# Six raw weight places instead of five, paid for by sharing two small tiles

## The chip, the cores and the metric

One Trainium2 chip, one of its cores. The metric is the device time of one launch in microseconds (us), median of the runs shown. Five engines run side by side, each through its own list of instructions: TensorE (PE; its weight loads are listed apart as PEld), VectorE (DVE), ScalarE (ACT), GpSimd (POOL) and SyncE (SP). In this kernel SP issues nearly all large loads from HBM, and 16 DMA engines carry them out.

## The reference

Two transformer blocks on 256 tokens of width 1024, in float32. The change lies in the last part of the first block, a mixture of 32 experts of which every token takes two:

```python
def expert_block(args):
    tok, wt, e = args
    xb = h_pad[tok]
    y = (jax.nn.silu(xb @ w_gate[e]) * (xb @ w_up[e])) @ w_down[e]
    return y * wt[:, None]
```

`w_gate[e]` and `w_up[e]` are 1024 x 512, `w_down[e]` is 512 x 1024, so each expert brings 6 MB of weights. Before this part come the modulation, attention and Fourier mixing and the router. After it come four feed-forward layers, an attention with selected keys and a gated MLP, all with weights that are read once.

## The kernel before

**Stream and places.** All weights are one list, `self.stream`, cut into pieces of at most 1 MB. `load` (L57 to L70) issues a piece from SP into a tile `raw` of the pool `rawp`. That pool has `RAW` = 5 places of 8 KB in each partition. `run_loads` (L78 to L82) decides how far ahead loads go:

```python
while self.loaded < len(self.stream) and self.loaded < self.free + RAW:
    self.load()
```

`self.free` is the first piece that is not yet done with its place. Pieces become done through `finished`, and `free` moves only over a run of done pieces. A piece that is held long therefore also holds back the loads that lie `RAW` places behind it, even if pieces after it are done. Which place a new piece gets is chosen when the program is built: the one that comes free earliest. SP runs its list in order, so a load that waits for its place holds up all loads behind it.

**Two ways of using a piece.** Most pieces are cut in two numbers of lower precision: ACT copies `raw` into `wh` (`high`, L104), DVE subtracts to get `wl` (`low`, L113), and the piece is finished. PE then multiplies with `wh` and `wl`. There are four pairs of `wh`/`wl` and one more pair (`whx`/`wlx`) in this stage. One piece of every expert, the second half of `w_down` (`NATIVE`), is not cut. PE multiplies with `raw` itself, and the place comes free only when these matmuls are done (`raw_done`).

**The expert stage.** Six pieces belong to an expert, in the order in which they are loaded: two of `w_gate` of expert e, two of `w_down` of expert e-1 (the second is the uncut one), two of `w_up` of expert e. In `moe` the order on PE, ACT and DVE is written out by hand (`tc.manual_schedule`). One pass e of the loop has on PE: first half of gate (`rows(e, 0, 0)`), the transposes of the up product of expert e-1 (`turn(1)`), `place`, second half of gate, `scatter` of expert e-2, both halves of down of expert e-1, first half of up, two pieces of `gather` (for e below 28 only), the transposes of the gate product (`turn(0)`), second half of up. The product of 64 slots x 512 comes out of PSUM as a copy by ACT (`leave`, L1517) into a tile `gu0` for gate or `gu1` for up, one buffer each. `turn` reads that tile on PE, and `total` on DVE adds what it left in PSUM. The product of silu(gate) and up is cut into `act` (two buffers), which `down` reads.

**The branch ahead of it.** Between the router and the expert stage there is a branch for experts with more than 64 tokens (`overflow`). SP reads a number for it (`TENSOR_LOAD most`, L1383) and waits there until the router has it. Loads behind the branch in SP's list cannot be issued earlier. The branch is not taken with these inputs.

**Elsewhere** the order on the engines is set by a scheduler, and the same `load` and `run_loads` feed the weights.

Of the kernel before, what the change touches and what calls it, by code (L numbers as in the profile page):

```python
# [10 lines left out]
F32 = mybir.dt.float32  # L11
F32R = mybir.dt.float32r
# [6 lines left out]
P = 128  # L19
# [1 line left out]
D = 1024  # L21
EPS = 1e-6
PIECE = 2048
RAW = 5
SX = 1
NEG = -1e30
SEL = -3e38
# [2 lines left out]
class Net:  # L30
    def __init__(self, ctx, tc, I, out):
        self.ctx, self.tc, self.nc, self.I, self.out = ctx, tc, tc.nc, I, out
        self.cp = self.pool(ctx, "const", 1)
        self.rawp = self.pool(ctx, "raw", RAW)
        self.psp = ctx.enter_context(tc.tile_pool(name="psum", bufs=4, space=PSUM))
# [42 lines left out]
    def run_loads(self):  # L78
        while self.free in self.done:
            self.done.discard(self.free)  # L80
            self.free += 1
        while self.loaded < len(self.stream) and self.loaded < self.free + RAW:  # L82
            self.load()
# [771 lines left out]
    def first(self):  # L855
# [3 lines left out]
        with ExitStack() as ctx:  # L859
# [171 lines left out]

            A, rec = {}, {}

            def scores(hd, t):
# [15 lines left out]
                nc.vector.scalar_tensor_tensor(p[0], p[1], st[:, 3, 1:2], p[0], op0=OP.mult, op1=OP.add)  # L1050
                A[hd, t] = p[0]

            def a_tr(hd, t):
                ps = self.bank().rearrange("p (k n) -> p k n", k=4)
                for kt in range(4):
                    nc.tensor.transpose(ps[:, kt, :], A[hd, t][:, P * kt : P * kt + P], self.idf)
                aT = at.tile([P, 4, P], F32, name="aT", bufs=2)
                nc.scalar.copy(aT, ps)
                A[hd, t] = aT

            O = {}

            def av(hd, t):
                if hd == 0:
                    O[t] = self.bank("acc").rearrange("p (h n) -> p h n", h=4)
                aT = A.pop((hd, t))
                for kt in range(4):
# [386 lines left out]
    def moe(self):  # L1454
        nc, tc, I = self.nc, self.tc, self.I
        self.limit = self.moe_end
        with ExitStack() as ctx:
            mp = self.pool(ctx, "moe", 1)
            self.extend(self.pool(ctx, "splitx", SX))
            XG, G, GT, gt, gu, act, ys, acc = {}, {}, {}, {}, {}, {}, {}, {}  # L1460

            def hot(g):
                G[g] = mp.tile([P, T, 4, P], F32R, name="G", bufs=2)
                for t in range(T):
                    nc.vector.tensor_tensor(G[g][:, t], self.slots[:, None, :].to_broadcast([P, 4, P]),
                                            self.posm[:, t, 4 * g : 4 * g + 4, None].to_broadcast([P, 4, P]),
                                            op=OP.is_equal)
# [16 lines left out]
            def place(e):  # L1484
                ps = gt[e] = self.bank().bitcast(F32R)
                for t in range(T):
                    nc.tensor.transpose(ps[:, P * t : P * t + P],
                                        G[e // 4][:, t, e % 4, :], self.idr)

            def grown(e):  # L1490
                ps = gt.pop(e)
                GT[e] = mp.tile([P, 256], F32R, name="GT", bufs=2)
                nc.scalar.copy(GT[e], ps[:, :256])
# [15 lines left out]
            def rows(e, which, q):  # L1509
                if q == 0:  # L1510
                    pr[which] = self.bank()
                product(pr[which], XG[e // 4][:, e % 4], None, piece(e, 2 * which + q), 4, 4 * q, 7)

            def leave(e, which):

                sb = mp.tile([P, 512], F32, name=f"gu{which}", bufs=1)
                nc.scalar.copy(sb.rearrange("s (a p) -> s a p", a=4), pr[which].rearrange("s (p a) -> s a p", a=4))  # L1517
                gu[which] = sb

            def turn(which):  # L1520
                tu[which] = self.bank()
                for a in range(4):
                    o = slice(P * a, P * a + P)
                    nc.tensor.transpose(tu[which][:, o], gu[which][:, o], self.idf)  # L1524

            def total(which):
                z[which] = mp.tile([P, 4, 64], F32, name=f"sum{which}", bufs=1)
                nc.vector.tensor_reduce(z[which], tu[which].rearrange("p (a i s) -> p a s i", a=4, i=2), axis=AX.X, op=OP.add)

            def down(e, q):  # L1530
                if q == 0:
                    pd[0], pd[1] = self.bank(), self.bank()
                w = piece(e, 4 + q)
                for half in range(2):
                    product(pd[half], act[e], None, w, 2, 2 * q, 3, slice(512 * half, 512 * half + 512))

            def yhigh(e, half):
                yh[half] = mp.tile([P, 512], F32R, name="yh", bufs=2)
                nc.scalar.activation(yh[half], pd[half], AF.Copy, scale=self.gslot[:, e : e + 1])

            def ylow(e, half):
                yl = mp.tile([P, 512], F32R, name="yl", bufs=2)
                nc.vector.scalar_tensor_tensor(yl, pd[half], self.gslot[:, e : e + 1], yh[half].bitcast(F32),  # L1543
                                               op0=OP.mult, op1=OP.subtract)
                ys.setdefault(e, []).append((yh[half], yl))

            def scatter(e):
                order = [(t, half) for half in range(2) for t in range(T)]
                for t, half in sorted(order) if e == 31 else order:
                    if e == 0:  # L1550
                        acc[t, half] = self.bank("acc")
                    for i in range(2):
                        self.mm(acc[t, half], GT[e][:, P * t : P * t + P], ys[e][half][i],
                                start=e == 0 and i == 0, stop=e == 31 and i == 1)
                del ys[e]
# [8 lines left out]
            def cut(which, e, n):  # L1564

                if (e, n) in names:
                    k = names.index((e, n)) + 1
                    while made[which] < k:
                        (self.low if which else self.high)()
                        made[which] += 1  # L1570
# [13 lines left out]
            with tc.manual_schedule(engines={mybir.EngineType.PE, mybir.EngineType.Activation, mybir.EngineType.DVE}):  # L1584
                for e in range(34):
                    new, old, last = e < 32, 0 < e < 33, e > 1
                    if new:
                        rows(e, 0, 0)
                    if old:
                        leave(e - 1, 1)  # L1590
                        nc.scalar.activation(z[0], z[0], AF.Silu)
                        cut(1, e - 1, 4)
                        turn(1)
                        place(e - 1)
                    cut(0, e, 2)
                    if old:
                        total(1)
                        nc.vector.tensor_mul(z[0], z[0], z[1])
                    if new:
                        rows(e, 0, 1)  # L1600
                    if old:
                        grown(e - 1)
                        A = act[e - 1] = mp.tile([P, 4, P], F32R, name="act", bufs=2)
                        self.split(A[:, :, :64], A[:, :, 64:], z[0])
                    if e % 4 == 0 and 0 < e < 28:
                        hot(e // 4 + 1)
                    cut(0, e, 3)
                    cut(1, e, 2)
                    if last:
                        scatter(e - 2)  # L1610
                    if new:
                        leave(e, 0)
                    if old:
                        down(e - 1, 0)
                    cut(0, e + 1, 0)
                    cut(1, e, 3)
                    if old:
                        down(e - 1, 1)
                    cut(0, e + 1, 1)
                    cut(1, e + 1, 0)  # L1620
                    if old:
                        self.raw_done()
                        for half in range(2):
                            yhigh(e - 1, half)
                            ylow(e - 1, half)
                    if new:
                        rows(e, 1, 0)
                    cut(0, e, 4)
                    cut(1, e + 1, 1)
                    if e < 28:  # L1630
                        for i in range(2):
                            gather(e // 4 + 1, 2 * (e % 4) + i)
                    if new:
                        turn(0)
                        total(0)
                        rows(e, 1, 1)
# [105 lines left out]
```

## Time and profile before

| | |
|---|---|
| Median of 3 runs | 1897.24 us (1896.63 to 1899.16) |
| Profiled execution, its own time | 1900.3 us |
| its span in the trace | 1898.6 us |
| PE busy | 1822.9 us, 96% |
| DVE busy | 1335.2 us, 70% |
| ACT busy | 1155.3 us, 61% |
| Expert stage, 237 to 760 us | 523 us: PE 505.27, DVE 448.07, ACT 409.60 us busy, DMA engines 0.95 of the time, 367 GB/s |
| A stretch of the second block, 900 to 1100 us | 200 us: PE 199.60, DVE 134.94, ACT 117.74 us busy, DMA engines 0.51, 170 GB/s |

The shares of busy time are averages over stages. The expert stage is one of heavy loads (367 GB/s), the second block is one of matmuls (PE busy all the time). The engine lists run in order, so an idle time in a list is ended by the thing that its next instruction waited for. The profile names this releaser.

### The profile page before, as it was taken

What the parts mean: (1) busy time and instruction counts of PE and PEld (TensorE: products, weight loads), DVE (VectorE), ACT (ScalarE), POOL (GpSimd) and SP (SyncE); (2) the same over time, 40 slices, a digit from 0 to 9 for tenths busy, and PEclk for the clock granted to TensorE, in tenths of its full rate; (3) what the DMA queues carried; (4) which work ended last, traced back from release to release, by engine and by line L of the source; (5) the groups of instructions that cost most, each with busy time, mean ns of one, the idle gap of its engine ahead of it and who ended that gap; (6) DMA issues with size and microseconds to landing.
All of it is one profiled execution on the core that took longest, in us unless ns stands there. A gap on an engine that the chain in (4) does not pass through costs nothing.

```text
span 1898.6 us, 23007 instructions
## 1 busy us (share of the span) xinstructions
PE 1822.9 (96%) x8305; PEld 1444.0 (76%) x8305; DVE 1335.2 (70%) x2114; ACT 1155.3 (61%) x1912; POOL 40.1 (2%) x73
## 2 busy tenths in 40 slices
PE   5999799999999999899999999999999999999998
PEld 2777577777777776688888888887888888887886
DVE  6887788888888888855577765556555776765554
ACT  6555588787777777744465664446444755465443
POOL 1000000000000000000000000000000010100000
PEclk8999799999999999999999999999999999999999
DMA  9774299999999999655564455555555555665551
GB/s 325 256 271 168 74 365 366 360 356 368 367 374 361 366 375 376 232 187 186 181 210 171 155 176 180 178 199 185 176 180 197 181 178 191 216 210 196 177 179 42
DMA packets 189268, 450.51 MB, mean 237 GB/s; under 512 B 9904, under 2 KB 118840, under 8 KB 164576
## 3 DMA queue, kind: packets, MB, share of 16 engines
q1 hardware_dynamic: 185056, 437.25, 64.3%
q0 software_dynamic: 3808, 11.25, 2.1%
q8 instruction: 66, 1.08, 0.2%
q10 hardware_dynamic: 288, 0.52, 0.1%
q14 instruction: 50, 0.41, 0.1%
HBM read 447.91 MB, written 1.07 MB: 236 GB/s over the span
## 4 chain that ended last, share of the span: by engine, by line
PE 72%; DMA 8%; ACT 5%; DVE 3%; issue 1%; SPq 0%; ACTq 0%; DVEq 0%
PE bank_w L161 51%; PE bank_acc L161 18%; DMA raw<-w_up 6%; ACT wh L104 2%; DMA raw<-w_down 2%; DVE wl L113 1%; PE bank_w L316 1%; PE bank_w L1524 1%; ACT wh L169 1%; PE bank_w L247 0%; ACT xh L250 0%; ACT XG L1482 0%; PE bank_w L719 0%; DVE yl L1543 0%; ACT L192 0%
## 5 line engine op out<-in xcount | busy, mean ns | idle before, releaser
L170 DVE TENSOR_TENSOR wl<-raw,wh 128x512 fp32r<-128x512 f32 (+3 forms) x814 | 522.9, 703 | 250.8 <-ACT wh L169 250.1
L169 ACT CAST wh<-raw 128x512 fp32r<-128x512 f32 (+3 forms) x814 | 461.1, 635 | 267.4 <-PE bank_w L161 204.0
L161 PE MATMUL bank_w<-wh,xh 128*128 128x512 f32 (+2 forms) x1056 | 407.0, 386 | 4.1 <-ACT xh L250 3.4
L161 PE MATMUL bank_w<-wh,xl 128*128 128x512 f32 (+2 forms) x1056 | 402.9, 382 | 0.9 <-DVE xl L251 0.9
L161 PE MATMUL bank_w<-wl,xh 128*128 128x512 f32 (+2 forms) x1056 | 402.5, 381 | 0.0
L104 ACT CAST wh<-raw 128x2048 fp32r<-128x2048 f32 x124 | 236.7, 1910 | 97.8 <-DMA raw<-w_up 47.5
L113 DVE TENSOR_TENSOR wl<-raw,wh 128x2048 fp32r<-128x2048 f32 x124 | 280.7, 2284 | 3.2 <-ACT wh L104 3.1
L161 PEld LDWEIGHTS bank_w<-wh,xh 128*128 128x128 f32 x1056 | 199.4, 189 | 42.7 <-ACT xh L250 6.3
L161 PEld LDWEIGHTS bank_w<-wh,xl 128*128 128x128 f32 x1056 | 199.1, 189 | 37.6 <-DVE xl L251 2.1
L161 PEld LDWEIGHTS bank_w<-wl,xh 128*128 128x128 f32 x1056 | 199.5, 189 | 35.1 <-issue 0.2
L161 PE MATMUL bank_w<-wh,XG 128*128 128x512 f32 x388 | 169.8, 438 | 0.0
L161 PE MATMUL bank_w<-wl,XG 128*128 128x512 f32 x388 | 152.3, 392 | 0.0
L161 PE MATMUL bank_acc<-wh,th 128*128 128x512 f32 x352 | 144.2, 410 | 0.0
L161 PE MATMUL bank_acc<-wh,tl 128*128 128x512 f32 x352 | 138.1, 392 | 0.0
L161 PE MATMUL bank_acc<-wl,th 128*128 128x512 f32 x352 | 137.9, 392 | 0.0
L309 ACT ACTIVATE silu<-bank_w,rs 128x256 f32<-128x256 f32 x88 | 41.7, 474 | 153.7 <-PE bank_w L161 153.5
L311 DVE SCALAR_TENSOR_TENSOR hid<-bank_w,rs,silu 128x256 f32<-128x256 f32 x88 | 42.6, 484 | 117.5 <-ACT silu L309 114.3
L161 PE MATMUL bank_w<-raw,act 128*128 128x512 f32 x256 | 115.0, 592 | 0.0
L161 PEld LDWEIGHTS bank_w<-wl,XG 128*128 128x128 f32 x388 | 73.1, 188 | 19.9 <-issue 7.2
L161 PEld LDWEIGHTS bank_w<-wh,XG 128*128 128x128 f32 x388 | 73.0, 188 | 19.9 <-issue 7.4
L161 PEld LDWEIGHTS bank_w<-raw,act 128*128 128x128 f32 x256 | 48.4, 189 | 48.5 <-issue 46.0
L161 PEld LDWEIGHTS bank_acc<-wh,tl 128*128 128x128 f32 x352 | 66.1, 188 | 14.1
(416 smaller groups left out, 2619.6 us busy)
## 6 DMA issues: line engine op xcount, KB each, us to landing
raw<-ffn_w_in SPq DMA_DIRECT2D x176, 512.0 KB, 4.9
raw<-w_gate SPq DMA_DIRECT2D x64, 1024.0 KB, 8.1
raw<-w_up SPq DMA_DIRECT2D x64, 1024.0 KB, 8.9
raw<-w_down SPq DMA_DIRECT2D x64, 1024.0 KB, 7.0
raw<-ffn_w_out SPq DMA_DIRECT2D x44, 1024.0 KB, 5.4
raw<-w_ada SPq DMA_DIRECT2D x16, 1024.0 KB, 5.7
raw<-a_w_in SPq DMA_DIRECT2D x12, 1024.0 KB, 5.9
raw<-b_w_in SPq DMA_DIRECT2D x12, 1024.0 KB, 5.3
```

The lines of the kernel that those rows point to most:

```text
L104: self.nc.scalar.copy(wh[:, :k], self.pieces[i][:, :k])
L113: self.nc.vector.tensor_sub(wl[:, :k], raw[:, :k], wh[:, :k].bitcast(F32))
L161: self.nc.tensor.matmul(*a, **k)
L169: self.nc.scalar.copy(h, src)
L170: self.nc.vector.tensor_sub(l, src, h.bitcast(F32))
L309: nc.scalar.activation(s, ps[:, :256], AF.Silu, scale=self.rs[t])
L311: nc.vector.scalar_tensor_tensor(hid[c, t], ps[:, 256:], self.rs[t], s, op0=OP.mult, op1=OP.mult)
L316: nc.tensor.transpose(ps[:, r, :], hid[c, t][:, P * r : P * r + P], self.idf)
L1524: nc.tensor.transpose(tu[which][:, o], gu[which][:, o], self.idf)
```

## The change

`RAW` becomes 6, so the pool `rawp` gets one more place. Room for it comes from two smaller tiles of the expert stage: the copies of gate and up (`leave`) go into one tile `gu0` with one buffer, and `act` has one buffer instead of two.

```diff
-RAW = 5
+RAW = 6
@@ leave
-                sb = mp.tile([P, 512], F32, name=f"gu{which}", bufs=1)
+                sb = mp.tile([P, 512], F32, name="gu0", bufs=1)
@@ the loop over e
-                        A = act[e - 1] = mp.tile([P, 4, P], F32R, name="act", bufs=2)
+                        A = act[e - 1] = mp.tile([P, 4, P], F32R, name="act", bufs=1)
```

The number of instructions on each engine stays as it was, and PE, ACT, DVE and POOL keep their order but for one pair of DVE instructions in the first block. What moves is on SP. Ahead of the branch stand the loads for the first experts, and the branch itself reads `most`. In the following piece of the difference a minus is before and a plus is now:

```order
 L66 DMA raw<-w_gate 128x2048 x2
 L66 DMA raw<-w_down 128x2048 x2
-L66 DMA raw<-w_up 128x2048
+L66 DMA raw<-w_up 128x2048 x2
 L1383 TENSOR_LOAD most
 L1383 ISA x2
 L1384 COMPARE_AND_BRANCH
```

The second `w_up` piece of expert 1 has moved ahead of the branch; before, it was the first load behind it.

In the steady part of the expert stage SP's loads stand in the same order, but wait for other places. Brackets name the engine whose progress a load waits for (DVE_49 is DVE, Activation_49 ACT, PE_49 PE, DMAHW an earlier load by the same counter). Six successive loads before:

```order
L66 DMA raw<-w_up 128x2048 [waits DMAHW2_49,PE_49]
L66 DMA raw<-w_up 128x2048 [waits DMAHW5_49,DVE_49]
L66 DMA raw<-w_gate 128x2048 [waits DMAHW6_49,DVE_49,Activation_49]
L66 DMA raw<-w_gate 128x2048 [waits DMAHW7_49,DVE_49]
L66 DMA raw<-w_down 128x2048 [waits DMAHW1_49,DVE_49,Activation_49]
L66 DMA raw<-w_down 128x2048 [waits DMAHW2_49,DVE_49]
```

The same six now:

```order
L66 DMA raw<-w_up 128x2048 [waits DMAHW4_49,DVE_49]
L66 DMA raw<-w_up 128x2048 [waits DMAHW2_49,PE_49]
L66 DMA raw<-w_gate 128x2048 [waits DMAHW5_49,DVE_49]
L66 DMA raw<-w_gate 128x2048 [waits DMAHW6_49,DVE_49,Activation_49]
L66 DMA raw<-w_down 128x2048 [waits DMAHW7_49,DVE_49]
L66 DMA raw<-w_down 128x2048 [waits DMAHW1_49,DVE_49,Activation_49]
```

The waits have moved down by one load: the place of the uncut piece (the wait for PE) is taken by the second `w_up` load, where the first one took it. By the places in the built program, in 24 of 31 experts before the first `w_up` waits for PE and now in 23 the second.

On ACT the copies out of PSUM keep their places in the list. Before, in one pass (`gu1` is the copy of up, `gu0` that of gate):

```order
L1517 COPY gu1_2313<-bank_w_2262 128x512 [waits PE_49,Activation_49]
L1591 ACTIVATE sum0_2294<-sum0_2294 128x256 [waits DVE_49,Activation_49]
L104 CAST wh_2327<-raw_2250 128x2048 [waits DMAHW7_49]
L1493 COPY GT_2341<-bank_w_2324 128x256 [waits PE_49]
L169 CAST act_2343<-sum0_2294 128x4x64 [waits DVE_49]
```

And now:

```order
L1517 COPY gu0_2315<-bank_w_2264 128x512 [waits PE_49,Activation_49]
L1591 ACTIVATE sum0_2296<-sum0_2296 128x256 [waits DVE_49]
L104 CAST wh_2329<-raw_2250 128x2048 [waits DMAHW7_49]
L1493 COPY GT_2343<-bank_w_2326 128x256 [waits PE_49]
L169 CAST act_2345<-sum0_2296 128x4x64 [waits DVE_49]
```

The copy of up now goes into `gu0` as well, and `act` is cut at the same point of the list.

## Rows read from the trace of the kernel before

**Rows 1.** The page: span and busy time of each engine (us, share, instructions).

```profile
span 1898.6 us, 23007 instructions
PE 1822.9 (96%) x8305; PEld 1444.0 (76%) x8305; DVE 1335.2 (70%) x2114; ACT 1155.3 (61%) x1912; POOL 40.1 (2%) x73
```

**Rows 2.** Busy time by stretch: length, engines (us), PE clock, DMA share, GB/s.

```profile
100.00:150.00 50.00, 50.00 (x215) 35.81 (x214) 42.99 (x72) 29.43 (x59) 1.28 (x2) 1.00 0.77 269
...
243.64:709.89 466.25, 453.00 (x2000) 337.18 (x1998) 400.46 (x311) 365.88 (x378) 0.57 (x1) 1.00 0.94 366
709.89:761.02 51.13, 47.59 (x200) 34.20 (x199) 42.82 (x33) 38.12 (x36) 0.00 (x0) 1.00 0.96 375
...
900.00:1100.00 200.00, 199.60 (x982) 166.70 (x981) 134.94 (x322) 117.74 (x262) 4.50 (x6) 1.00 0.51 170
```

**Rows 3.** PE in order of time: start, length, first matmul on an uncut piece.

```profile
243.64 0.59 PE L161 MATMUL bank_w<-raw,act 128*128 128x512 f32 x1
...
401.19 1.02 PE L161 MATMUL bank_w<-raw,act 128*128 128x512 f32 x2
...
417.64 0.59 PE L161 MATMUL bank_w<-raw,act 128*128 128x512 f32 x1
...
709.89 0.59 PE L161 MATMUL bank_w<-raw,act 128*128 128x512 f32 x1
```

**Rows 4.** Busy time by stretch: one expert period, and ten microseconds.

```profile
407.73:424.18 16.45, 16.45 (x76) 12.50 (x75) 14.72 (x12) 13.64 (x15) 0.00 (x0) 1.00 0.99 382
...
303.00:313.00 10.00, 10.00 (x47) 7.97 (x46) 8.56 (x8) 8.16 (x11) 0.00 (x0) 1.00 1.02 424
```

**Rows 5.** Waits, 243 to 710 us: who waited for whom, us in total, times, longest.

```profile
ACT wh L104 <- DMA raw<-w_up: 41.3, 31, 2.7
DVE act L170 <- ACT act L169: 38.6, 27, 2.7
ACT wh L104 <- DMA raw<-w_down: 27.4, 21, 2.5
ACT wh L104 <- DMA raw<-w_gate: 18.5, 26, 1.9
DVE yl L1543 <- ACT yh L1539: 13.2, 21, 1.8
...
PE bank_w L161 <- ACT XG L1482: 8.0, 9, 1.5
```

**Rows 6.** ACT in order of time: the cut of the first w_up piece, twice.

```profile
411.93 1.91 ACT L104 CAST wh<-raw 128x2048 fp32r<-128x2048 f32 x1 [1.08 <-DMA raw<-w_up]
...
428.85 1.92 ACT L104 CAST wh<-raw 128x2048 fp32r<-128x2048 f32 x1 [1.56 <-DMA raw<-w_up]
```

**Rows 7.** DVE in order of time, around the cut of act in two passes.

```profile
414.45 0.43 DVE L170 TENSOR_TENSOR act<-sum,act 128x256 fp32r<-128x256 f32 x1 [1.08 <-ACT act L169]
...
431.37 0.43 DVE L170 TENSOR_TENSOR act<-sum,act 128x256 fp32r<-128x256 f32 x1 [1.55 <-ACT act L169]
431.71 1.28 DVE L1465 TENSOR_TENSOR G<-slots,posm 128x512 fp32r<-128x512 f32 x2
```

**Rows 8.** SP's queue in order of time: issue of loads, start and length of the pair.

```profile
201.87 32.84 SPq L66 DMA_DIRECT2D raw<-w_up  x2
...
409.34 3.09 SPq L66 DMA_DIRECT2D raw<-w_gate  x2
417.14 2.49 SPq L66 DMA_DIRECT2D raw<-w_down  x2
421.27 0.80 SPq L66 DMA_DIRECT2D raw<-w_up  x2
425.64 3.08 SPq L66 DMA_DIRECT2D raw<-w_gate  x2
```

**Rows 9.** Tile raw, 243 to 710 us: time from a load's issue to its landing.

```profile
DMA to landing us min/median/max: 4.9/7.8/10.9
```

**Rows 10.** The chain that ended last, in the expert stage: start, length, what.

```profile
421.27 7.56 DMA raw<-w_up
```

## What the change should do to the time

> **What bounds the kernel now.** I read the page first, then busy time by stretch, then the expert stage alone: its waits, the lists of PE, ACT and DVE in order of time, and SP's queue. The page says PE is busy 96% of 1898.6 us [rows 1], which hides two kinds of stretch. In the second block PE is busy 199.60 of 200 us while the DMA engines carry 170 GB/s [rows 2]: there a load that comes earlier can bring nothing. In the expert stage the loads run at 366 GB/s, and PE stands still for 466.25 - 453.00 = 13.25 us of 27 expert periods [rows 2].
>
> Busy time understates what PE loses there, since a matmul that follows a stall is drawn longer. A better measure is the time from one expert's first uncut matmul to the next expert's. The first of them starts at 243.64 us and the 28th at 709.89 us, so 27 periods take 466.25 us, 17.27 us each. One of them, from 401.19 to 417.64 us, takes 16.45 us [rows 3]; four others take as little, and in 16.45 us counted from another point, 407.73 us, PE is busy throughout [rows 4]. These periods hold the same matmuls as the rest, so 16.45 us is what PE needs and 0.82 us per period is lost.
>
> Who takes it is seen one engine back. In those 27 periods ACT waits for loads: 41.3 us for w_up, 27.4 for w_down, 18.5 for w_gate [rows 5], together 87.2 us or 3.2 us per expert. PE feels only the part that exceeds the slack of ACT's list. In the pass at 412 us ACT waits 1.08 us for the first w_up piece, in the next one 1.56 us [rows 6]. Directly behind it DVE waits 1.08 and 1.55 us for the cut of act [rows 7], which in ACT's list stands behind that w_up cut. The two numbers agree, so the 38.6 us that DVE waits there [rows 5] are the same delay handed on.
>
> Why the loads are late is seen in SP's queue. The second w_gate load goes out at 409.34 + 3.09 - 0.33 = 412.1 us (0.33 us is one issue), and the next load, w_down, only at 417.14 us [rows 8]. That is 5 us without an issue, while a load lands after 4.9 us at best and 7.8 us in the middle [rows 9], so the engines run nearly dry. Then four loads follow within 5 us, and the first w_up piece, issued at 421.27 us, lands 7.56 us later [rows 10], too late for ACT by the 1.56 us above. SP is waiting for places, not for the engines. A closed loop is what bounds the stage: a place comes free, the load takes 8 us, ACT cuts late, DVE cuts late, the next place comes free late.
>
> **The change, part by part.**
>
> *The sixth place in the expert stage.* As the change section shows, every load now waits for the release that the load before it waited for. In the pass above the first w_down load moves from 417.14 to about 412.1 us, the second from 419.3 to 417.1, the first w_up load from 421.27 to 419.3, the second from 421.7 to 421.3, and the w_gate pair from 425.64 and 428.4 to about 421.7 and 425.6 [rows 8]. ACT could have used the first w_up piece at 428.85 - 1.56 = 427.3 us [rows 6]. Issued at 419.3 us it lands at 427.1 us if it takes the median 7.8 us, and at 424.2 us if it takes the least, 4.9 us [rows 9]. The stretch without an issue is filled, so the queue in front of it is shorter, and I expect something between: 0.2 to 3 us in time instead of 1.56 us late. Each of the other pieces gains 0.4 to 5 us. ACT's waits for loads should shrink from 3.2 to under 1 us per expert, and the period then falls to PE's own.
>
> What is next late is PE at 16.45 us. DVE is busy 400.46 / 27 = 14.83 us per period and ACT 365.88 / 27 = 13.55 us [rows 2]. The loads are 6 x 1.049 = 6.29 MB per expert, which the engines moved at 424 GB/s for 10 us [rows 4], so 14.8 us. All three lie under 16.45 us. The upper end of the gain is 27 x 0.82 = 22.1 us, the lower one PE's drawn idle time, 13.25 us. I take nearly the upper, because the same instructions have been seen in 16.45 us, and leave 0.1 us per period for the passes in which DVE also builds G (1.28 us [rows 7], once in four experts): 27 x 0.72 = **19.4 us**.
>
> *The last three periods*, without gather, take 51.13 us with PE busy 47.59 us [rows 2]. The bounds are 0 and the 3.5 us in which PE stands still. I take **3 us**, near the upper end as above.
>
> *The load that moves ahead of the branch.* The second w_up piece of expert 1 is issued today at 201.87 + 32.84 - 0.33 = 234.4 us, its partner at 201.87 us [rows 8]. Now it goes at about 201.87 us, into a time of idle DMA engines. SP's reading of most stands behind it and waits for the router either way. That takes 1 MB out of the busy stage, 2.5 us at 424 GB/s [rows 4]. But PE's first period is among the short ones, so its worth lies between 0 and 2.5 us. I take 0.
>
> *The shared tiles.* The copy of gate into gu0 must now wait until PE has transposed the copy of up, and the copy of up until PE has transposed that of gate. In PE's list turn(1) stands ahead of the second half of gate, whose result the first copy waits for anyway, and turn(0) ahead of the second half of up, which the second copy waits for. With one act the cut waits for down of the expert before. Its input comes from turn(1), which stands behind that down in PE's list. So each new wait has ended before an old wait of the same instruction can end. The cost is nothing, whatever ACT's timing.
>
> *The rest.* In the first block the sixth place lets loads go earlier, but PE is busy 50.00 of 50 us at 100 to 150 us [rows 2]. In the second block nothing waits for loads. I take 0, with 1.5 us to either side.
>
> The sum is 19.4 + 3 = 22.4 us. Against the profiled execution's own 1900.3 us that makes 1877.9 us. That execution lies 3.1 us above the median of the runs, so in the terms of the median it is 1897.24 - 22.4 = 1874.8, or **1875 us**. The best case is 22.1 + 3.5 + 2.5 + 1.5 = 29.6 us, so 1868 us.
>
> **The rivals.**
>
> *The DMA engines become the bound.* Their share already reads 0.94 to 0.96 in the two expert stretches [rows 2]. If 375 GB/s, the better of the two rates, is what they can hold, a period cannot fall below 6.29 / 375 = 16.78 us. The gain is then 27 x 0.49 = 13 us, and the time 1884 us. If 366 GB/s is the ceiling, a period stays at 17.2 us and the time at about 1895 to 1897 us. Against it: the engines held 382 GB/s over a whole period and 424 GB/s over 10 us [rows 4], the first at a share of 0.99 and the second at 1.02, so a share near 1 does not say that no more can be moved. The Trainium skill, "DMA: Bandwidth & Descriptors", section Specifications, states a limit of about 358 GB/s from HBM per core and a vendor's derated 368 GB/s. By that rule the stage would be at its ceiling and the change worth nothing (about 1897 us), but the trace's 382 GB/s over 16.45 us speaks against it. Chance 0.17, 0.11 of it at 1884 us.
>
> *DVE's list takes PE's place.* If DVE's waits for act and for yh (38.6 and 13.2 us [rows 5]) were of its own order and stayed, a period would need 14.83 + 1.43 + 0.49 = 16.75 us. The gain is then 27 x 0.52 = 14 us, and the time 1883 us. Against it: the equal numbers in the lists of ACT and DVE [rows 6, 7]. Chance 0.10.
>
> *The waits of ACT cost nothing.* If PE's losses come from the copies XG (8.0 us [rows 5]) and from banks instead of late weights, earlier loads only let ACT wait elsewhere, and the time stays 1897 us. Against it: 8.0 us is a third of what is lost, and XG's copies stand in ACT's list behind a late cut too. Chance 0.07.
>
> *Slower.* One more 1 MB load in flight stands before the small loads that POOL issues in the first block. At 100 to 150 us the engines are already used 0.77 [rows 2]. Each small load that something waits for could come up to 2.5 us later. About four such moments would make 10 us, and with the gain of the expert stage lost at a DMA ceiling the time would be 1907 us. The point from which it decides is a PE wait for such a load, and in that stretch PE has none. Chance 0.04.
>
> **How the numbers follow.** The forecast (1868 to 1880 us) gets 0.62, the rivals 0.17, 0.10, 0.07 and 0.04. A measurement of this kernel can tell about 0.2%, 3.8 us. Faster by more than that are the forecast, the DMA rival at 1884 us and the DVE rival: 0.62 + 0.11 + 0.10 = 0.83. Same: 0.06 + 0.07 = 0.13. Slower: 0.04. A range from 1868 us, the best case, to 1888 us, which leaves the two cases at 1883 and 1884 us as much room above as the forecast has, holds 0.83 less a little for each case's own spread, about 0.8.
>
> **What would show it.** If the steps are right, ACT's waits for loads in the stage fall under a third of 87 us, DVE's wait for act under 20 us, the 27 periods lie near 16.5 us with PE busy nearly all the time, and the loads run above 380 GB/s. Landing times may well grow, as loads are issued earlier and stand in line. SP shows the second w_up load at about 202 us. If periods stay at 16.8 us or more with ACT still waiting for loads, the DMA rival holds. If ACT no longer waits and PE still does, one of the next two holds. A wait of ACT's copies gu for PE's transposes would refute the part on the shared tiles.

## The result, and the profile after

The changed kernel takes 1871.51 us (median of four runs, 1870.52 to 1874.24), against 1896.93 us for the kernel before on the same chip. The ratio is 0.9865, with a 95% interval of 0.985 to 0.988, so the change made the kernel 25.4 us faster. The profiled execution took 1874.24 us with a span of 1872.5 us, which is 26.1 us under the span of before [rows 1]. Ratios, here and below, leave out two executions of the first experiments that took 3715 and 4721 us.

The page first, with the span and the busy time of each engine (us, share of the span, instructions):

```profile
span 1872.5 us, 22794 instructions
PE 1809.4 (97%) x8305; PEld 1443.0 (77%) x8305; DVE 1335.0 (71%) x2114; ACT 1149.1 (61%) x1912; POOL 40.1 (2%) x73
```

PE is busy 13.5 us less than before with the same 8305 matmuls. In the two expert stretches below it is 10.1 us (453.00 to 444.08 and 47.59 to 46.42 us); there it is the drawn length of matmuls behind a stall, which the prediction warned of. The other 3.4 us lie outside and were not followed. Of 26.1 us saved, busy time thus shows half as work that went away.

Busy time by stretch, cut at the same matmuls as [rows 2] (length; PE, PEld, DVE, ACT and POOL busy; PE clock; DMA share; GB/s). The first line holds 27 expert periods, the second the three without gather, the third the period that came out longest:

```profile
243.96:688.84 444.88, 444.08 (x1999) 337.66 (x1998) 401.01 (x311) 362.00 (x379) 0.57 (x1) 1.00 0.98 383
688.84:735.26 46.42, 46.42 (x199) 34.52 (x198) 43.54 (x34) 35.97 (x36) 0.00 (x0) 1.00 1.01 409
...
506.88:524.51 17.63, 16.83 (x75) 12.57 (x74) 15.27 (x12) 14.41 (x15) 0.00 (x0) 1.00 0.99 390
```

The 27 periods fell from 466.25 to 444.88 us, 16.48 us each. PE stood still for 0.80 us of them instead of 13.25. Twenty-six periods take 16.41 to 16.45 us, one takes 17.63 us. The last three fell from 51.13 to 46.42 us, and PE has no gap there. DVE and ACT did the same work as before. The loads run at 383 GB/s instead of 366, and at 409 instead of 375 in the last three.

The waits in the 27 periods (who waited for whom, us in total, times, longest), to be held against [rows 5]:

```profile
ACT gu L1517 <- PE bank_w L161: 43.9, 27, 1.7
ACT yh L1539 <- PE bank_w L161: 20.6, 24, 1.0
...
DVE act L170 <- ACT act L169: 13.6, 27, 1.3
...
DVE yl L1543 <- ACT yh L1539: 10.1, 20, 1.8
...
ACT wh L104 <- DMA raw<-w_gate: 4.1, 7, 1.9
ACT wh L104 <- DMA raw<-w_up: 1.8, 2, 1.3
```

ACT's 87.2 us of waits for loads are now 5.9 us. What ACT waits for instead is PE: the copy of a product (gu) and the scaled copy of down's (yh) are ready to run before their matmuls have ended. A helper that waits for the engine it serves is a sign that the served engine is the bound. The gu copies wait for the product (L161). None waits for the transposes of the shared tile (L1524).

The pass in which the prediction followed each load, now on SP (issue, length of the pair), and PE's uncut multiplies beside it:

```profile
402.00 5.53 SPq L66 DMA_DIRECT2D raw<-w_down  x2
409.37 2.86 SPq L66 DMA_DIRECT2D raw<-w_up  x2
412.35 3.64 SPq L66 DMA_DIRECT2D raw<-w_gate  x2
```

```profile
408.28 3.59 PE L161 MATMUL bank_w<-raw,act 128*128 128x512 f32 x8
424.73 3.59 PE L161 MATMUL bank_w<-raw,act 128*128 128x512 f32 x8
```

Counted from the uncut multiply, the first w_up load goes out 409.37 - 408.28 = 1.1 us behind it. Before, it was 421.27 - 417.64 = 3.6 us behind it [rows 3, 8]. So it is 2.5 us earlier, and ACT's wait of 1.56 us for it [rows 6] is gone.

The lines for the one thing that moved ahead of the branch, and for landing:

```profile
197.59 4.33 SPq L66 DMA_DIRECT2D raw<-w_up  x2
```

```profile
DMA to landing us min/median/max: 4.9/8.0/11.7
```

The second w_up load of expert 1 is issued at 197.59 + 4.33 - 0.33 = 201.6 us, against 234.4 us before. Loads take a little longer to land than in [rows 9], since they are asked for earlier and stand in line.

### The profile page after: what moved, and what is told of

It is laid out like the page before. It is cut to its first block, busy times and chain, and to the rows that moved or that the text cites. A ratio compares the mean times of both kernels' runs of the same rounds, so it can differ in the third digit from the quotient of the medians.

```text
span 1872.5 us, 22794 instructions
## 1 busy us (share of the span) xinstructions
PE 1809.4 (97%) x8305; PEld 1443.0 (77%) x8305; DVE 1335.0 (71%) x2114; ACT 1149.1 (61%) x1912; POOL 40.1 (2%) x73
## 4 chain that ended last, share of the span: by engine, by line
PE 83%; ACT 3%; DVE 2%; issue 1%; DMA 1%; ACTq 0%; DVEq 0%; SPq 0%
PE bank_w L161 59%; PE bank_acc L161 20%; PE bank_w L1524 1%; PE bank_w L316 1%; ACT wh L169 1%; DMA raw<-w_gate 1%; PE bank_w L247 0%; ACT xh L250 0%; PE bank_w L719 0%; ACT L192 0%; DVE wl L113 0%; ACT wh L104 0%; ACT L309 0%; PE bank_w L1487 0%; PE bank_w L507 0%
## 5 line engine op out<-in xcount | busy, mean ns | idle before, releaser
L161 PE MATMUL bank_w<-wh,xh 128*128 128x512 f32 (+2 forms) x1056 | 406.4, 385 | 4.1 <-ACT xh L250 3.4
L161 PE MATMUL bank_w<-wh,xl 128*128 128x512 f32 (+2 forms) x1056 | 402.7, 382 | 0.9 <-DVE xl L251 0.9
L161 PE MATMUL bank_w<-wl,xh 128*128 128x512 f32 (+2 forms) x1056 | 402.5, 381 | 0.0
L161 PEld LDWEIGHTS bank_w<-wh,xh 128*128 128x128 f32 x1056 | 199.2, 189 | 42.5 <-ACT xh L250 6.5
L161 PEld LDWEIGHTS bank_w<-wh,xl 128*128 128x128 f32 x1056 | 199.1, 189 | 37.5 <-DVE xl L251 2.2
L161 PEld LDWEIGHTS bank_w<-wl,xh 128*128 128x128 f32 x1056 | 199.1, 189 | 35.0 <-issue 0.2
L161 PE MATMUL bank_w<-wh,XG 128*128 128x512 f32 x388 | 169.8, 438 | 0.0
L161 PE MATMUL bank_w<-wl,XG 128*128 128x512 f32 x388 | 152.2, 392 | 0.0
L161 PE MATMUL bank_acc<-wh,th 128*128 128x512 f32 x352 | 144.2, 410 | 0.0
L161 PE MATMUL bank_acc<-wh,tl 128*128 128x512 f32 x352 | 138.0, 392 | 0.0
L161 PE MATMUL bank_acc<-wl,th 128*128 128x512 f32 x352 | 137.7, 391 | 0.0
L161 PE MATMUL bank_w<-raw,act 128*128 128x512 f32 x256 | 115.0, 592 | 0.0
L161 PEld LDWEIGHTS bank_w<-wl,XG 128*128 128x128 f32 x388 | 73.1, 189 | 19.8 <-DVE wlx L113 5.3
L161 PEld LDWEIGHTS bank_w<-wh,XG 128*128 128x128 f32 x388 | 73.0, 188 | 20.0 <-issue 7.4
L161 PEld LDWEIGHTS bank_w<-raw,act 128*128 128x128 f32 x256 | 48.4, 189 | 48.5 <-issue 46.0
L161 PEld LDWEIGHTS bank_acc<-wh,tl 128*128 128x128 f32 x352 | 66.1, 188 | 14.1
```

The lines of the kernel that those rows point to most:

```text
L161: self.nc.tensor.matmul(*a, **k)
```

## Experiments

The first two ask which half of the change did it. The next ones ask what bounds the stage before and after. Each ratio is to runs of the kernel before made beside that experiment, whose medians lie between 1896.75 and 1899.30 us.

**The sharing alone, with five places.** The two lines of the change that free memory, without the place that they pay for:

```diff
 RAW = 5
-                sb = mp.tile([P, 512], F32, name=f"gu{which}", bufs=1)
+                sb = mp.tile([P, 512], F32, name="gu0", bufs=1)
-                        A = act[e - 1] = mp.tile([P, 4, P], F32R, name="act", bufs=2)
+                        A = act[e - 1] = mp.tile([P, 4, P], F32R, name="act", bufs=1)
```

> Five places as before, but gate and up share gu0 and act has one buffer: the half of the change that is not the sixth place. Theory (the places bound the expert stage, sharing is free, since PE's list already puts each new wait ahead of an old one): as before, 1897 us within 2 us, 27 periods of 17.2 to 17.3 us, ACT waiting for loads 80 to 95 us in them. Rival (part of the gain comes from the sharing or from the shifted tiles): 1872 to 1890 us.

Measured: 1898.05 us, ratio 0.9995 (0.9976 to 1.0013). The waits of ACT in about 27 periods:

```profile
ACT wh L104 <- DMA raw<-w_up: 37.6, 27, 2.3
ACT wh L104 <- DMA raw<-w_down: 30.0, 21, 2.4
ACT wh L104 <- DMA raw<-w_gate: 19.6, 27, 2.3
```

They add up to 87.2 us, as before. Within that interval sharing costs nothing and brings nothing, so the gain belongs to the place.

**Five places, but the long-held piece loaded last.** The uncut half of w_down is held until PE has multiplied with it. Here the stream brings it as the last of an expert's six pieces, so that it arrives later and keeps its place for less time. Tiles are as before.

```diff
-            for n, w in ((0, "w_gate"), (4, "w_down"), (2, "w_up")):
-                if n == 4 and e:
+            for n, w in ((0, "w_gate"), (4, "w_down"), (2, "w_up"), (5, "w_down")):
+                if n >= 4 and e:
```

> Five places and no sharing, but the uncut half of w_down is loaded last of its expert's six pieces instead of fourth, so it holds its place for two loads (about 5 us) less. Theory (what counts is places times the time for which each is held): most of the gain without a sixth place; each w_up load waits for the release that the load before it waited for, the gate and w_down loads wait as before with fewer loads ahead of them, so 1872 to 1884 us, 1876 as the middle. Rival (what counts is how many loads are in flight or how deep the queue is, five against six): 1893 to 1898 us.

Measured: 1884.26 us, ratio 0.9929 (0.9908 to 0.995), 12.6 us off. That is a hair past the upper end of what was expected, and far from the rival's 1893 us. ACT's waits in about 27 periods:

```profile
ACT whx L104 <- DMA raw<-w_gate: 27.3, 26, 2.5
ACT wh L104 <- DMA raw<-w_down: 23.0, 17, 2.6
...
ACT wh L104 <- DMA raw<-w_gate: 16.4, 27, 1.2
```

The 37 to 41 us of waits for w_up have left the list, and part of them came back at w_gate. A change of order alone, with the same number of places, gives half the gain. So the number of places is not all that counts.

Why only half is seen in the times of issue, counted from an expert's first uncut multiply (medians over the experts of each trace). The first w_up load goes out 3.6 us behind it before, and 1.1 us behind it both in this run and in the changed kernel. But the next w_down load goes out 0.2 us ahead of it before, 1.1 us in this run and 6.3 us in the changed kernel, and the first load of the w_gate pair ahead of that 8.6, 8.5 and 12.4 us. The order moves the w_up loads as far as the sixth place does, and hardly moves the others. From its issue to the end of its multiplies the uncut piece stays 16.0 us instead of 18.6, so 2.6 us less and not the 5 us of the expectation. The run does not separate this shorter stay from the earlier turn of the w_up loads, which now stand ahead of the uncut piece.

**Six places, and the same order.** The same edit on the changed kernel.

> The changed kernel (six places, shared tiles) with the uncut half of w_down loaded last. Theory (PE is the bound of the expert stage once the places suffice): nothing more to gain, 1869 to 1873 us, periods of 16.41 to 16.45 us. Rival (places still bind): clearly under 1868 us.

Measured: 1870.94 us, ratio 0.9864 (0.9839 to 0.9889), no different from the change alone. The 27 periods in one line, columns as above:

```profile
244.40:688.10 443.70, 443.70 (x1999) 337.59 (x1998) 401.06 (x311) 362.08 (x379) 0.57 (x1) 1.00 0.98 384
```

PE has no gap at all, and the one long period is gone as well, which makes 443.70 us of 444.88. Loads that come still earlier bring nothing: PE's matmuls are the bound after the change.

**Less work for PE, with six places and with five.** If PE is the bound after and the loop of places before, taking work from PE must pay in the one and not in the other. The edit is the same in both:

```diff
-                    for i in range(2):
+                    for i in range(1):
                         self.mm(acc[t, half], GT[e][:, P * t : P * t + P], ys[e][half][i],
-                                start=e == 0 and i == 0, stop=e == 31 and i == 1)
+                                start=e == 0 and i == 0, stop=e == 31 and i == 0)
```

> The changed kernel, but scatter multiplies only the high part of y: four of its eight matmuls per expert are left out (0.226 us each), the low part is still computed by DVE. Theory (PE is the bound now, the next ones are DVE at 14.8 us and the loads at 14.8 us per period): each period falls by 0.90 us to about 15.53 us, so 29 us less, 1842 to 1848 us. Rival (DMA engines or DVE already bind at 16.4 us): no shorter than 1865 us.

> The kernel before with five places, and of the scatter's eight multiplies in each expert the four of the low part are left out (the low part of y is thus missing from the sum; everything that loads, cuts or copies weights stands as before). The same edit on the changed kernel took 21.6 us from the expert stage (484.08 us between the first and the last uncut multiply, against 505.67). Theory: with five places the stage is bound by the loop of load, cut and release, in which these multiplies have no part, so little of their time comes back: 5 to 15 us, 1882 to 1892 us, the waits for loads on ScalarE (87 us in the 27 periods before) growing by about what TensorE saves. Rival: TensorE's own work is the bound with five places as well and the waits only lie in its shade: the whole 29 us comes back, or at least the 21.6 of the changed kernel, 1868 to 1875 us.

Measured: 1855.82 us with six places (0.9786, 0.9758 to 0.9814) and 1899.34 us with five (1.0014, 1.0 to 1.0028). The stage from the first expert's first uncut multiply to the last expert's, in the changed kernel, then with less work and six places, then with less work and five, from three traces:

```profile
243.96:749.63 505.67, 502.84 (x2247) 380.52 (x2246) 455.24 (x358) 407.71 (x431) 0.57 (x1) 1.00 0.98 384
```

```profile
244.41:728.49 484.08, 479.07 (x2124) 357.63 (x2123) 453.29 (x359) 409.02 (x432) 0.58 (x1) 1.00 1.00 400
```

```profile
245.00:773.70 528.70, 495.96 (x2124) 356.76 (x2123) 455.06 (x358) 413.25 (x432) 0.58 (x1) 1.00 0.95 367
```

With five places the stage gives back 3 us of its 531.7 (243.64 to 775.37 us), the loads keep their 367 GB/s, and PE now idles for 33 us. This is the clearest sign of the loop: 29 us of matmuls were taken away and the time did not move. It saved even less than the 5 us that the theory asked for. The theory was wrong in a detail too. It had ACT's waits for loads grow from 87 us, and they are 82.5 us over nearly 28 periods; the idle time shows on PE:

```profile
ACT wh L104 <- DMA raw<-w_up: 40.4, 30, 2.1
...
ACT wh L104 <- DMA raw<-w_down: 23.0, 17, 2.5
ACT wh L104 <- DMA raw<-w_gate: 19.1, 28, 2.1
```

With six places 505.67 us become 484.08, so 21.6 of the 29 us come through, fewer than expected. PE stands still for 5 us, and periods that had been 16.4 us are mostly 15.5 but 16.1 to 16.3 in one of four, the one right behind DVE's building of G. In each of those six the gather waits about 0.2 us for yl:

```profile
297.24 0.74 PE L161 MATMUL bank_w<-G,xl 128*128 128x256 f32 x4 [0.21 <-DVE yl L1543]
```

So there DVE's list is the next to bind. ACT's waits for loads in the stage also grew, from 7.0 to 11.9 us, at a DMA share of 1.00; how much of the missing 7 us is theirs was not separated. Another 2.1 us went behind the stage, where the clock's mean over the next 150 us was lower, 0.97 against 0.99 (the first line is this run, the second the changed kernel):

```profile
728.50:878.50 150.00, 143.44 (x623) 114.12 (x622) 89.25 (x183) 77.37 (x161) 2.14 (x5) 0.97 0.57 188
```

```profile
749.60:900.00 150.40, 145.24 (x639) 115.82 (x638) 90.64 (x185) 77.72 (x162) 2.13 (x5) 0.99 0.59 192
```

**Work moved from PE to ACT and DVE.** If PE bounds the stage, cutting one uncut piece in four should pay without leaving anything out.

```diff
-    NATIVE = ((0, 5), (1, 5), (2, 5), (3, 5))
+    NATIVE = ((0, 5), (2, 5), (3, 5))
```

> The changed kernel, but in one expert of four (the second of each four) the last half of w_down is cut in two like the others instead of being multiplied uncut. Nothing is left out of the result. In those eight experts the uncut half's multiplies become more but cheaper ones: by the trace of the changed kernel about 1.6 us less on TensorE, against 1.9 us more on ScalarE and 2.3 us more on VectorE. Theory: after the change TensorE's work is the bound of nearly every period (16.41 and 16.45 us, busy 444.1 of 444.9), with ScalarE at 362.0 and VectorE at 401.0 of 444.9, so the eight experts lose about 1.6 us each: 13 us off, 1858 to 1866 us (middle 1860). Rival: VectorE, which has 14.8 us in an average period, works through its list in order, and with 2.3 us more the period of a cut expert is set by it at about 17.1 us: eight times 0.65 us more, about 1877 us.

Measured: 1892.34 us (0.9971, 0.9959 to 0.9984), 21 us slower than the changed kernel. The rival had the right sign and a third of the size. A pair of periods around a cut expert, and the period behind it:

```profile
244.03:279.70 35.67, 33.49 (x149) 26.19 (x148) 32.48 (x25) 29.56 (x30) 0.00 (x0) 0.95 0.93 356
279.70:296.11 16.41, 16.41 (x75) 12.50 (x74) 14.56 (x14) 13.31 (x15) 0.00 (x0) 1.00 0.98 376
```

The pair takes 35.67 us instead of 16.41 + 16.45 = 32.86, and the next period is the old one again. DVE's list in the pass of the next such expert, and then PE's:

```profile
328.98 2.29 DVE L113 TENSOR_TENSOR wlx<-raw,whx 128x2048 fp32r<-128x2048 f32 x1
331.18 4.49 DVE L113 TENSOR_TENSOR wl<-raw,wh 128x2048 fp32r<-128x2048 f32 x2
335.59 1.41 DVE L1543 SCALAR_TENSOR_TENSOR yl<-bank_w,gslot,yh 128x512 fp32r<-128x512 f32 x2
```

```profile
336.39 1.22 PE L161 MATMUL bank_w<-G,xl 128*128 128x256 f32 x4 [2.71 <-DVE yl L1543]
```

The yl subtractions stand behind one subtraction more than in the changed kernel, and the gather's second bank comes free only with them. PE waits for yl in six such passes, 16.2 us in all, and in the first pass for ACT's copy XG (2.14 us). Around the wait PE's granted clock reads 0.76 over 7 us, and 1.00 again behind them:

```profile
333.30:340.30 7.00, 4.29 (x18) 3.71 (x17) 7.00 (x7) 3.04 (x4) 0.00 (x0) 0.76 0.99 383
340.30:348.50 8.20, 8.20 (x41) 6.78 (x39) 6.35 (x6) 6.95 (x8) 0.00 (x0) 1.00 0.85 314
```

So part of that stretch ran at 1.2 GHz instead of 2.4. It is the part behind the wait: the clock reads 0.99 over the 3.10 us up to the wait's end and 0.57 over the 3.90 us after it. The wait cost more than its length.

**The same, with yl ahead of the other subtraction in those passes.**

```diff
                     cut(0, e + 1, 1)
-                    cut(1, e + 1, 0)
+                    late = old and not self.native(e - 1, 5)
+                    if not late:
+                        cut(1, e + 1, 0)
...
                             ylow(e - 1, half)
+                    if late:
+                        cut(1, e + 1, 0)
```

> The changed kernel with the last half of w_down cut in one expert of four, as in the run before this one (1892.3 us), and in those eight passes the two subtractions for yl stand ahead of the subtraction for the next expert's first cut piece of w_gate on VectorE instead of behind it. Nothing is left out of the result. In the run before this one a pair of periods around a cut expert took 34.7 to 37.4 us instead of 32.9: the gather's multiplies waited 2.1 to 2.7 us for yl, which stood behind a 2.28 us subtraction, and TensorE ran at half speed for a few microseconds behind the wait. Theory: the place of yl in VectorE's list is the cause; with yl 2.3 us earlier the wait and the slow stretch go, and the 1.6 us that the cut saves on TensorE in each of eight experts shows: 1858 to 1866 us. Rival: the list is simply too long in that stretch (VectorE then has about 62 us of work in four periods, TensorE 64), and the 2.3 us show at another instruction, the sums of gate and up or the act: 1872 to 1890 us.

Measured: 1879.83 us (0.9904, 0.9887 to 0.9921). The place of yl was worth 12.5 of the 21 us. A pair around a cut expert:

```profile
246.35:279.80 33.45, 32.27 (x150) 24.85 (x149) 31.05 (x24) 28.22 (x30) 0.00 (x0) 1.00 0.95 358
```

It takes 33.45 us with no fall of the clock, but still 0.6 us more than without the cut, where 1.6 us less was hoped for. The rival holds for the rest. The subtraction shows up at the next things in DVE's list, and PE waits for them (244 to 730 us):

```profile
PE bank_w L161 <- DVE act L170: 5.4, 9, 0.9
PE bank_w L161 <- DVE yl L1543: 3.6, 7, 0.5
```

The first uncut multiply also starts 2.4 us later than in the changed kernel (246.35 against 243.96 us; the other traces have it between 243.64 and 245.12 us). I have not followed that. From there to the last expert's first uncut multiply it takes 511.45 us against 505.67, so 5.8 us of the loss lie in the stage.

**The same, with GpSimd doing the subtraction that stands ahead of yl.** GpSimd is idle in this stage, so DVE's list gets back its old length.

```diff
+                    self.by = nc.gpsimd if old and not self.native(e - 1, 5) else nc.vector
                     cut(1, e + 1, 0)
+                    self.by = nc.vector
```

> The changed kernel with the last half of w_down cut in one expert of four (1892.3 us alone, 1879.8 us with yl moved ahead in VectorE's list), and in those eight passes the subtraction for the next expert's first cut piece of w_gate, which stands ahead of yl, is done by GpSimd, which has nothing to do in this stage. Nothing is left out of the result. VectorE then has as much to do in the pass as in the changed kernel. Theory: the length of VectorE's list in the passes with a cut is all that is left; with it at its old length the 1.6 us less on TensorE come through in most of the eight passes: 1858 to 1866 us, and no wait of TensorE for yl or act. Rival: GpSimd takes so long for 128 x 2048 elements (no row shows it), or slows VectorE beside it so much, that the first multiplies of the next expert wait for its wl: 1875 to 1895 us.

Measured: 1919.08 us (1.0105, 1.0084 to 1.0127), slower than the kernel before and past the rival's range. GpSimd, DVE and PE in the same pass:

```profile
263.14 5.12 POOL L113 TENSOR_TENSOR wl<-raw,wh 128x2048 fp32r<-128x2048 f32 x1 [42.53 <-ACT wh L104]
```

```profile
263.74 6.68 DVE L113 TENSOR_TENSOR wlx<-raw,whx 128x2048 fp32r<-128x2048 f32 x1
270.34 1.40 DVE L1543 SCALAR_TENSOR_TENSOR yl<-bank_w,gslot,yh 128x512 fp32r<-128x512 f32 x2
```

```profile
271.13 0.92 PE L161 MATMUL bank_w<-G,xl 128*128 128x256 f32 x4 [4.89 <-DVE yl L1543]
```

GpSimd ends at 268.26 us, and DVE's subtraction, which takes 2.28 us elsewhere, ends at 270.42 us, 2.16 us behind it. It looks as if DVE stood still until GpSimd was done. The Trainium skill, "SBUF — State Buffer", section Who interferes with whom, says: "only the shared port pair causes contention, and it's an exclusive lock", between VectorE and GpSimd. The trace agrees: 6.68 us instead of 2.28, and the end one subtraction behind GpSimd's. So yl came later still, and PE waited 34.3 us for it in seven passes. Moving the work to an idle engine did not take it off DVE.

None of the versions that leave nothing out beats the changed kernel. Only the loading order with six places equals it, within the measurement.

## Why the prediction was right, and where its terms were off

The forecast was 1875 us, and 1871.5 us came out. The reason given holds: it is the sixth place that ends the waits for loads. The forecast of the gain was 3.7 us short of the 26.1 us between the spans, 2.0 us of it in the 27 periods and 1.7 us in the last three. Point by point:

- **What bounds the kernel before: a closed loop of places.** It held. Less work for PE with five places moved nothing, and the same loads in another order or with one more place did. One reading on the way to it was wrong. In the 5 us without an issue, 412.1 to 417.1 us, the engines did not run nearly dry but carried 428 GB/s from loads already issued, and both periods around that pass are short ones (16.45 and 16.41 us): the late cut cost PE nothing there. The loop is seen one pass on. DVE waits 1.55 us for the cut of act [rows 7] and then builds G, so the first of its next two subtractions ends only at 432.92 + 2.28 = 435.2 us. SP has waited 6.5 us for it and issues w_down at 435.26 us, and from 434.50 to 437.00 us the engines carry only 141 GB/s. The period from 434.06 us takes 17.21 us. From the trace of before, the engines in both stretches, DVE, SP, and what SP waited for from 243.64 to 710 us:

```profile
412.10:417.10 5.00, 5.00 (x25) 4.13 (x23) 3.77 (x5) 4.86 (x6) 0.00 (x0) 1.00 1.01 428
...
434.50:437.00 2.50, 2.50 (x7) 1.12 (x6) 2.50 (x2) 1.89 (x2) 0.00 (x0) 1.00 0.55 141
```

```profile
432.92 4.48 DVE L113 TENSOR_TENSOR wl<-raw,wh 128x2048 fp32r<-128x2048 f32 x2
```

```profile
435.26 2.75 SPq L66 DMA_DIRECT2D raw<-w_down  x2
```

```profile
SPq L66 <- DVE wl L113: 353.1, 103, 7.1
SPq L66 <- PE bank_w L161: 39.5, 27, 2.9
```

- **27 periods, 19.4 us taken, bounds 13.25 and 22.1.** Measured 466.25 - 444.88 = 21.4 us. The 0.1 us per period set aside for the passes in which DVE builds G was not needed: they take 16.41 to 16.45 us like the rest. What keeps the gain from the full 22.1 us is one period of 17.63 us, in which two loads came late (ACT waited 1.92 us for a w_gate piece, yl came late, and PE waited 0.80 us). With the uncut piece loaded last that period too is short. PE's 16.45 us as the next bound was right. So was the choice of the period between equal matmuls over busy time, which would have given 13.25 us.
- **The last three periods, 3 us taken, bounds 0 and 3.5.** Measured 51.13 - 46.42 = 4.7 us, above the bound. This is the term that was mis-sized. The bound was PE's drawn idle time, the very measure that the first paragraphs had rejected for the other periods. The right bound was to be had from the trace of before: the three periods have no gather, whose eight multiplies follow one another in 423.85 - 422.90 = 0.95 us there. So 3 x (16.45 - 0.95) = 46.5 us was the floor and 4.6 us the gain. The trace of after has 46.42 us.

```profile
422.90 0.64 PE L161 MATMUL bank_w<-G,xh 128*128 128x256 f32 x4
423.37 0.65 PE L161 MATMUL bank_w<-G,xl 128*128 128x256 f32 x4
423.85 0.60 PE L1524 MATMUL bank_w<-idf,gu 128*128 128x128 f32 x4
```

- **The load ahead of the branch, 0 taken.** It goes out at 201.6 us as said, and the first uncut multiply came at 243.96 us instead of 243.64. No gain.
- **The shared tiles, 0 taken.** Shown by the run with the sharing alone, and by the gu copies, which wait for products only.
- **The rest, 0 with 1.5 us to either side.** From the last expert's first uncut multiply (775.37 us before, 749.63 us after) to the end of the span it takes 1123.2 us before and 1122.9 us after. The sum of the terms is 21.4 + 4.7 - 0.3 + 0.3 = 26.1 us, which is the difference of the spans.
- **The signs.** ACT's waits fell under a third (5.9 of 87 us), DVE's wait for act to 13.6 us, the loads rose to 383 GB/s, and landing grew a little, all as named.
- **The DMA rival.** It is refuted: it asked for periods of 16.78 us or more. The engines carried 383 GB/s over 445 us, 409 over 46 us, and 400 over 484 us with less work for PE. The figures of 358 and 368 GB/s that the prediction drew from the Trainium skill, "DMA: Bandwidth & Descriptors", section Specifications, are no ceiling here; the measurement decides.
- **The DVE rival.** For the change itself it is refuted: the periods of 16.41 to 16.45 us lie under the 16.75 us that it asked for, and DVE's wait for act fell with ACT's waits for loads. But DVE stands close behind PE: in the runs with one more cut piece, a subtraction more in a pass cost more than the PE time that it saved.
- **The rivals "ACT's waits cost nothing" and "slower".** Neither showed. ACT's waits went and PE's gaps with them, and the time behind the stage stayed the same.

## What to carry to other kernels

When loads stop and then come in bursts, look at what the issuing engine waits for before counting GB/s: one more place, or loading the piece that is held long behind the others, moves loads earlier without any faster transfer. Check that the engines really run low in the gap, since loads already issued can fill it. Measure what the busy engine loses by the period between equal instructions, also in the short stretches at the end, since busy time hides stalls. Before moving work off the engine that has become the bound, look for what stands behind the moved instruction in the other engine's list, and which of its results the bound engine takes at once.

## What the runs showed of the hardware

- One core's loads held 400 GB/s over 484 us at a DMA share of 1.00, and 409 GB/s over 46 us at a share of 1.01, while 367 GB/s already read 0.95. The share is no measure of how much more can be moved.
- A subtraction of 128 x 2048 elements took 2.28 us on DVE and 5.1 us on GpSimd, and a DVE subtraction that met GpSimd's took 6.68 us. Spans on GpSimd are rough in the profile.
- Around a PE wait of 2.71 us its granted clock read 0.76 over 7 us (0.57 over the 3.90 us behind the wait), and 1.00 again behind them. With a wait of 0.5 us at the same place it read 1.00 over the whole pair of periods.
